# The seven products of the last feed-forward matrix: order of sums, casts and transfers

## Chip, cores and metric

The kernel runs on one core of a Trainium2 chip. The metric is device time in microseconds, from three runs of each kernel; one more execution was profiled.

## What is computed

One decoder layer on x (1024 tokens by 1024), with the float32 products each made of three passes over two parts of the operands.

```python
def rms_norm(x, g):
    y = x * rsqrt(mean(x * x, axis=-1, keepdims=True) + EPS)
    return y * g

def swiglu(x, w_in, w_out):
    a, b = split(x @ w_in, 2, axis=-1)
    return (silu(a) * b) @ w_out

h = x
h = h + stick_breaking_attention(rms_norm(h, norm_mix), sb_w_in, sb_w_out)
h = h + swiglu(rms_norm(h, norm_ffn), ffn_w_in, ffn_w_out)
gate = sigmoid(rms_norm(h, norm_ple) @ ple_w_gate)
h = h + gate * (p @ ple_w_proj)
out = rms_norm(h, final_norm)
```

The change lies in the product with `ffn_w_out` (2816 by 1024), the sum into h behind it, and the start of the product with `ple_w_gate`.

## The kernel before

Activations are kept transposed, 128 features on the partitions and tokens along the row. A float32 operand is used as two parts: the *high* part is a cast to fp32r on ScalarE, the *low* part is the value less the high part, a subtraction on VectorE or GpSimd. `mm3` (L118) makes a product of three matmuls: high by high (L119), high by low (L120), low by high (L121).

The product with `ffn_w_out` is made as one step of a fast two-by-two scheme: seven products P1, P5, P6, P7, P2, P4, P3 (`FO`, L611), in this order, instead of eight. A product takes sums and differences of quarters of the matrix and of the activations, and has 11 pieces along the inner dimension (`NJ`), so there are 77 pieces, numbered n (`NS`). A piece is a 128 by 1024 tile: 512 columns of weights beside 512 of activations. Each piece is used by 12 matmuls of 512 columns (four row blocks, three parts), which add into four banks of PSUM.

From here on the order on each engine is that in which the program is written (`manual_schedule`, L608). Step n of the loop (L1071) writes, in this order:

- `fo_load(n + 6)` (L622): two transfers on SyncE's queue, weights (L620) and activations (L642), 256 KB each. Buffers of `NG` = 7 names rotate; in P4 three of them (`4 + j % 3`), since the others are about to hold the residual stream.
- `fo_lo(n + 2)` (L675): the difference of piece n+2 on VectorE (L684; L682 in P1).
- `fo_hi(n + 3)` (L644): for P5, P6 and P7 the sum or difference of quarters on VectorE, 128 by 1024 (L652), for P4 and P3 of one half only, none for P1 and P2; then the cast on ScalarE (L672; L670 in P1).
- at steps of P2 that `gate_split` lists, `w_split` (L90) of a gate weight: the cast (L100) on ScalarE and the difference (L102) on VectorE, for the last three weights on GpSimd; at steps that `gate_load` lists, `w_load` (L82) of a gate weight on SyncE's queue (L87). Raw gate weights alternate between two buffers.
- the matmuls of piece n, and one or two *jobs* from a list.

The high and low parts of pieces and of the later gate weights come from a pool of 16 tiles (`xp`, tag "X"), two of which are taken all the time.

Jobs are added at a product's last piece. `evac_fo` (L1039) takes a product's four banks into the residual stream `hres`: P1 and P5 with copies on ScalarE (L1044, L1046), the others with additions on VectorE (L1034); P7 has three of them for each bank. `residual` (L1036) is a transfer on GpSimd's queue that adds 256 KB of the stream before the feed-forward part into `hres`: four behind P6, twelve behind P7. After P2 and P4, `parts3(m, 0)` (L1014) is a job for each of eight row blocks: it casts the block, scaled by the gain, on ScalarE (L1022), takes the difference on VectorE (L1023), squares the block on ScalarE (L1029; L1026 for the first) and adds the square to `acc3` (L1031), on VectorE for odd m and on GpSimd for even m.

After the loop: the gate weights that are not yet split (`w_next`, L107: load, split, two further loads, a split ahead), and for the first 512 tokens the gate products (L1163), eight row blocks of 24 matmuls; in the first block `parts3(m, 1)` of the second half for four m, and the sums of squares (`stats_sum`, L124), whose result is spread over the partitions by transposes on TensorE (L149) after the second block, before the first gate block can be finished.

Of the kernel before, what the change touches and what calls it, by code (L numbers as in the profile page):

```python
# [34 lines left out]
def f(ap):  # L35
    return ap.bitcast(F32)
# [3 lines left out]
def tile_trunk(ctx: ExitStack, tc: tile.TileContext, xT, pT, gains, ident, w_qkv, w_o, w_fi, w_fo, w_g, w_p, outT):  # L40
# [46 lines left out]
            nc.sync.dma_start(t[:, :n, :], src)  # L87
            raws[k] = t

    def w_split(k):  # L90
        if k < lim[0] and k in raws:
            n = order[k][1]
            t = raws.pop(k)
            if len(order[k]) > 2 and order[k][2]:
                hi = xp.tile([P, T], F32R, name=f"whi{k}", tag="X").rearrange("p (k m) -> p k m", k=KT)
                lo = xp.tile([P, T], F32R, name=f"wlo{k}", tag="X").rearrange("p (k m) -> p k m", k=KT)
            else:
                hi = wp.tile([P, KT, P], F32R, name=f"whi{k}", tag="whi", bufs=2)
                lo = wp.tile([P, KT, P], F32R, name=f"wlo{k}", tag="wlo", bufs=2)
            nc.scalar.copy(hi[:, :n, :], t[:, :n, :])  # L100
            eng = nc.gpsimd if k < N1 or k >= len(order) - 3 else nc.vector
            eng.tensor_tensor(lo[:, :n, :], t[:, :n, :], f(hi[:, :n, :]), op=ALU.subtract)  # L102
            parts[k] = (hi, lo)

    cur = [0]

# [498 lines left out]
    def tmp(name):  # L605
        return pt.tile([P, 512], F32, name=name, tag="t")
# [403 lines left out]
        return hh[h][kt][:, cs], hl[h][kt][:, cs]  # L1010

    begun = set()

    def parts3(m, h):  # L1014
        hs = HS[h]
        g = gn[:, 2, m:m + 1]
        if h or m < 7:
            d = p3.tile([P, 2, 512], F32R, name=f"g_{m}_{h}", tag=f"s{m}" if h else f"g{m}", bufs=1)
        else:
            d = duo(xp, "g_7_0", "X", None)  # L1020
        hh[h][m], hl[h][m] = d[:, 0, :], d[:, 1, :]
        nc.scalar.activation(hh[h][m], hres[m][:, hs], AF.Copy, scale=g)  # L1022
        nc.vector.scalar_tensor_tensor(hl[h][m], hres[m][:, hs], g, f(hh[h][m]), op0=ALU.mult, op1=ALU.subtract)  # L1023
        if h not in begun:
            begun.add(h)
            nc.scalar.activation(acc3[:, hs], hres[m][:, hs], AF.Square)  # L1026
        else:
            s = tmp("sq")
            nc.scalar.activation(s, hres[m][:, hs], AF.Square)  # L1029
            eng = nc.vector if m % 2 else nc.gpsimd  # L1030
            eng.tensor_tensor(acc3[:, hs], acc3[:, hs], s, op=ALU.add)  # L1031

    def plus(out, x, y, op=ALU.add):
        nc.vector.tensor_tensor(out, x, y, op=op)  # L1034
# [4 lines left out]
    def evac_fo(p, i, ps):  # L1039

        c11, c12 = hres[i][:, HS[0]], hres[i][:, HS[1]]
        c21, c22 = hres[i + 4][:, HS[0]], hres[i + 4][:, HS[1]]
        if p == "P1":
            nc.scalar.copy(c11, ps)  # L1044
        elif p == "P5":
            nc.scalar.copy(c22, ps)  # L1046
        elif p == "P6":
            plus(c21, ps, c11)
            residual(i, 0)
        elif p == "P7":  # L1050
            plus(c12, c21, c22, ALU.subtract)
            residual(i, 1)
            plus(c21, ps, c21, ALU.subtract)
            plus(c22, c21, c22)
            residual(i + 4, 1)
            residual(i + 4, 0)
        elif p == "P2":
            plus(c11, ps, c11)
        elif p == "P4":
            plus(c21, ps, c21)  # L1060
        else:
            plus(c12, ps, c12)

    gate_load = {("P6", 8): 0, ("P7", 4): 1, ("P2", 1): 2, ("P2", 3): 3, ("P2", 5): 4, ("P4", 1): 5, ("P4", 2): 6}
    gate_split = {("P2", 1): 0, ("P2", 3): 1, ("P2", 5): 2, ("P2", 7): 3, ("P2", 9): 4}
    n_wg = len(gate_split)
    jobs = []
    for n in (3, 4, 5):
        fo_load(n)
# [1 line left out]
    for n in range(NS):  # L1071
        p, j = FO[n // NJ], n % NJ
        fo_load(n + 6)
        if n < 3:
            nc.sync.dma_start(SX[n][:, 1, :], act_d[n][0])
        if 5 <= n < 5 + NJ:
            fo_w(SX[n - 5][:, 0, :], n - 5, 1, 1)
        fo_lo(n + 2)
        fo_hi(n + 3)
        if (p, j) in gate_split:  # L1080
            w_split(n_fi + gate_split[(p, j)])
        if (p, j) in gate_load:
            w_load(n_fi + gate_load[(p, j)])
        if j == 0:
            pm = [mb() for _ in range(4)]
        hi, lo = fop.pop(n)
        for i in range(4):
            ws = slice(i * P, i * P + P)
            mm3(pm[i], hi[:, 0, ws], lo[:, 0, ws], hi[:, 1, :], lo[:, 1, :], j == 0, j == NJ - 1)
        if n in (2, 5):  # L1090
            rests.pop(0)()
        if j == NJ - 1:
            jobs += [lambda p=p, i=i, ps=ps: evac_fo(p, i, ps) for i, ps in enumerate(pm)]
            more = {"P2": range(4), "P4": range(4, KT)}
            jobs += [lambda m=m: parts3(m, 0) for m in more.get(p, ())]
        elif j:
            left = NJ - 1 - j
            for _ in range(1 if len(jobs) <= left else 2):
                if jobs:
                    jobs.pop(0)()  # L1100
# [58 lines left out]
    for ri, (c0, n) in enumerate(ranges):  # L1159
# [3 lines left out]
        for m in range(KT):  # L1163
            wh, wl = wg[m]
            ple_load(ri * KT + m + 2)
            ps = mb()
            for kt in range(KT):
                mm3(ps[:, :n], wh[:, kt, :], wl[:, kt, :], *gx(kt, c0, n), kt == 0, kt == KT - 1)

            def evac(ri=ri, m=m, c0=c0, n=n, ps=ps):  # L1170
                evac_g(ps, m, c0, n, pls.pop(ri * KT + m), ri == last)
                if ri == last:
                    nc.scalar.activation(hg[m], hres[m][:, c0:c0 + n], AF.Copy, scale=gf[:, m:m + 1])

            held.append(evac)
            if (ri, m) == (0, 0):
                parts3(0, 1)
                parts3(1, 1)
                y3 = stats_sum(cp, mb(), [acc3[:, HS[0]], None], 0, 4)
                parts3(2, 1)  # L1180
                parts3(3, 1)
            elif (ri, m) == (0, KT - 1):
                y3 = stats_sum(cp, mb(), [None, acc3[:, HS[1]]], 512, 4)
            if ri < 2 and m == 1:
                stats_spread(mb(), y3, rstd3, 512 * ri, 4)
            if m or ri == last:
                while held:
                    held.pop(0)()
            if ri == 0 and 1 < m < 6:
                parts3(m + 2, 1)  # L1190
            if before is not None:
                b0, bn = before
                s = 4 if ri == last else 5
                if m == s - 2:
                    yfin = stats_sum(cp, mb(), acc4, b0, bn // P)
                elif m == s:
                    rfin = spread(yfin, bn // P)
                if m >= s:
                    for q in range(3 * (m - s), min(3 * (m - s) + 3, KT)):
                        fin(q, b0, bn, rfin)  # L1200
# [44 lines left out]
```

## Time and profile before

| | us |
|---|---|
| median of three runs | 1393.1 (1392.13 to 1393.51) |
| the profiled execution | 1391.86 |
| its span, first to last instruction | 1389.9 |
| TensorE busy | 1343.3 |
| VectorE busy | 1076.6 |
| ScalarE busy | 626.3 |
| GpSimd busy | 408.8 |
| mean granted clock of TensorE | 0.99 |

All times of rows are in microseconds from the span's start unless marked otherwise; PE is TensorE, DVE VectorE, ACT ScalarE, POOL GpSimd, SP SyncE (SPq and POOLq their queues). L12 is line 12 of the kernel. Matmuls overlap: a row of 0.39 us is followed by the next matmul 0.227 us later when nothing is missing. The granted clock is a share of full speed.

### The profile page before, as it was taken

What the parts mean: (1) busy time and instruction counts of PE and PEld (TensorE: products, weight loads), DVE (VectorE), ACT (ScalarE), POOL (GpSimd) and SP (SyncE); (2) the same over time, 40 slices, a digit from 0 to 9 for tenths busy, and PEclk for the clock granted to TensorE, in tenths of its full rate; (3) what the DMA queues carried; (4) which work ended last, traced back from release to release, by engine and by line L of the source; (5) the groups of instructions that cost most, each with busy time, mean ns of one, the idle gap of its engine ahead of it and who ended that gap; (6) DMA issues with size and microseconds to landing.
All of it is one profiled execution on the core that took longest, in us unless ns stands there. A gap on an engine that the chain in (4) does not pass through costs nothing. (4 is left out here: it accounts for less than half of the span.)

```text
span 1389.9 us, 17597 instructions
## 1 busy us (share of the span) xinstructions
PE 1343.3 (97%) x6506; PEld 1112.2 (80%) x6506; DVE 1076.6 (77%) x1379; ACT 626.3 (45%) x1091; POOL 408.8 (29%) x289
## 2 busy tenths in 40 slices
PE   9999999999999999999999999999999889888996
PEld 7888888888888888888888888888888667666896
DVE  6878878887887876687888888888896678667775
ACT  6666565556656754443232332232253325244433
POOL 2222231213223401245544454544420002002321
PEclk9999999999999999999999999999999999999998
DMA  5101110111111742532122221222168457761113
GB/s 187 58 16 61 46 47 31 46 46 46 46 47 61 252 180 91 175 122 82 57 89 91 91 91 61 77 91 91 61 228 308 147 176 207 221 243 50 34 66 109
DMA packets 65877, 146.98 MB, mean 106 GB/s; under 512 B 7168, under 2 KB 11648, under 8 KB 65792
## 3 DMA queue, kind: packets, MB, share of 16 engines
q1 hardware_dynamic: 61200, 134.06, 28.0%
q0 software_dynamic: 4320, 11.54, 3.3%
q8 instruction: 51, 0.84, 0.3%
q14 instruction: 34, 0.28, 0.1%
q10 hardware_dynamic: 272, 0.26, 0.1%
HBM read 114.38 MB, written 31.46 MB: 105 GB/s over the span
## 5 line engine op out<-in xcount | busy, mean ns | idle before, releaser
L413 DVE TENSOR_TENSOR_SCAN a<-a,hot 128x128 f32<-128x128 f32 (+7 forms) x128 | 193.1, 1524 | 21.9 <-ACT a L406 21.5
L119 PE MATMUL b_pj<-xh,whi 128*128 128x512 f32 x352 | 140.6, 399 | 0.0
L121 PE MATMUL b_pj<-xh,wlo 128*128 128x512 f32 x352 | 138.7, 394 | 0.4 <-POOL wlo L102 0.4
L120 PE MATMUL b_pj<-xl,whi 128*128 128x512 f32 x352 | 137.8, 392 | 0.0
L102 POOL TENSOR_TENSOR wlo<-wraw,whi 128x1024 fp32r<-128x1024 f32 x27 | 67.5, 2501 | 225.5 <-ACT whi L100 130.5
L436 DVE TENSOR_TENSOR al<-b_tp,ah 128x512 fp32r<-128x512 f32 (+2 forms) x160 | 93.2, 599 | 52.1 <-ACT ah L435 51.7
L435 ACT CAST ah<-b_tp 128x512 fp32r<-128x512 f32 (+2 forms) x160 | 81.9, 521 | 79.9 <-PE b_tp L426 79.1
L406 ACT ACTIVATE a<-b_z 128x128 f32<-128x128 f32 (+2 forms) x192 | 86.9, 490 | 49.2 <-PE b_z L404 48.2
L120 PE MATMUL b_m<-fl,fh 128*128 128x512 f32 x231 | 94.0, 407 | 11.2 <-DVE fl L684 11.0
L426 PE MATMUL b_tp<-hot,a 128*128 128x128 f32 x576 | 94.2, 273 | 2.5 <-DVE al L436 2.5
L426 PEld LDWEIGHTS b_tp<-hot,a 128*128 128x128 f32 x576 | 72.6, 140 | 25.8 <-DVE al L436 5.6
L121 PE MATMUL b_m<-fh,fl 128*128 128x512 f32 x231 | 91.8, 397 | 0.0
L119 PE MATMUL b_m<-fh 128*128 128x512 f32 x231 | 91.8, 397 | 0.0
L121 PEld LDWEIGHTS b_pj<-xh,wlo 128*128 128x128 f32 x352 | 66.0, 188 | 16.2 <-POOL wlo L102 0.5
L120 PEld LDWEIGHTS b_pj<-xl,whi 128*128 128x128 f32 x352 | 66.2, 188 | 8.9
L119 PEld LDWEIGHTS b_pj<-xh,whi 128*128 128x128 f32 x352 | 66.1, 188 | 8.6
L446 PE MATMUL b_av<-ah,V 128*128 128x512 f32 (+2 forms) x160 | 70.7, 442 | 0.0
L672 ACT CAST fh<-s 128x1024 fp32r<-128x1024 f32 x33 | 34.7, 1050 | 78.2 <-DVE s L652 65.8
L120 PEld LDWEIGHTS b_m<-fl,fh 128*128 128x128 f32 x231 | 44.2, 191 | 29.8 <-DVE fl L684 20.7
L684 DVE TENSOR_TENSOR fl<-s,fh 128x1024 fp32r<-128x1024 f32 x33 | 42.6, 1290 | 32.1 <-ACT fh L672 32.1
L672 ACT CAST fh<-raw 128x1024 fp32r<-128x1024 f32 x33 | 34.0, 1049 | 69.6 <-DVE raw L652 56.1
L894 ACT ACTIVATE sg<-u 128x512 f32<-128x512 f32 x22 | 13.9, 632 | 106.1 <-issue 91.4
(3066 smaller groups left out, 3883.4 us busy)
## 6 DMA issues: line engine op xcount, KB each, us to landing
fraw<-w_fi SPq DMA_DIRECT2D x44, 512.0 KB, 4.1
raw<-w_fo SPq DMA_DIRECT2D x56, 256.0 KB, 3.5
raw<-act SPq DMA_DIRECT2D x55, 256.0 KB, 3.6
wraw<-w_qkv SPq DMA_DIRECT2D x22, 512.0 KB, 3.5
sp<-hl SPq DMA_DIRECT2D x14, 512.0 KB, 3.1
act<-u SPq DMA_DIRECT2D x22, 256.0 KB, 2.2
act<-c SPq DMA_DIRECT2D x22, 256.0 KB, 2.6
s<-act SPq DMA_DIRECT2D x22, 256.0 KB, 5.4
```

The lines of the kernel that those rows point to most:

```text
L102: eng.tensor_tensor(lo[:, :n, :], t[:, :n, :], f(hi[:, :n, :]), op=ALU.subtract)
L119: nc.tensor.matmul(ps, whi, xhi, start=first, stop=False)
L120: nc.tensor.matmul(ps, whi, xlo, start=False, stop=False)
L121: nc.tensor.matmul(ps, wlo, xhi, start=False, stop=last)
L406: nc.scalar.activation(a[:, c0:c0 + e], z[:, :e], AF.Sigmoid, scale=-SCALE)
L413: nc.vector.tensor_tensor_scan(a[:, L - 1::-1], a[:, L - 1::-1], hot[:, back], 0.0, op0=ALU.mult, op1=ALU.max)
L426: nc.tensor.transpose(b[:, j * P:(j + 1) * P], a[:, kt * P:(kt + 1) * P], idn)
L435: nc.scalar.copy(ah[:, m0:m0 + 512 - j0 * P], b[:, j0 * P:])
L436: nc.vector.tensor_tensor(al[:, m0:m0 + 512 - j0 * P], b[:, j0 * P:], f(ah[:, m0:m0 + 512 - j0 * P]), op=ALU.subtract)
L446: nc.tensor.matmul(ps[:, c0:], o.V[:, kt, hd, :], ah[:, r0:], start=kt == 0, stop=False)
L672: nc.scalar.copy(hi, d)
L684: nc.vector.tensor_tensor(lo, d, f(hi), op=ALU.subtract)
```

## The change

Five edits, all in the seven products and the start of the gate stage:

- step n writes `fo_hi(n + 3)` ahead of `fo_lo(n + 2)`;
- `parts3` is cut in two: casts and squares on ScalarE, then difference and addition on VectorE (`parts3_lo`), which comes one job later, beside the casts of the next row block (`parts3_row`: five jobs for four blocks, nine pieces for the eight of the second half). All additions of squares are VectorE's;
- `residual(i, 1)` moves from P7's evacuation to P2's, `residual(i + 4, 1)` to P4's;
- the loads of gate weights stand further apart, five instead of seven in the stage; three weights instead of five are split in it, cast and difference one step apart; five instead of three weights have their difference on GpSimd;
- the first gate block takes the pieces of the second half from the same list.

```diff
-    def w_split(k):
+    def w_hi(k):
         if k < lim[0] and k in raws:
...
             nc.scalar.copy(hi[:, :n, :], t[:, :n, :])
-            eng = nc.gpsimd if k < N1 or k >= len(order) - 3 else nc.vector
+            parts[k] = (hi, lo, t)
+
+    def w_lo(k):
+        if k < lim[0] and k in parts and len(parts[k]) == 3:
+            n = order[k][1]
+            hi, lo, t = parts[k]
+            eng = nc.gpsimd if k < N1 or k >= len(order) - 5 else nc.vector
             eng.tensor_tensor(lo[:, :n, :], t[:, :n, :], f(hi[:, :n, :]), op=ALU.subtract)
             parts[k] = (hi, lo)
+
+    def w_split(k):
+        w_hi(k)
+        w_lo(k)
...
         nc.scalar.activation(hh[h][m], hres[m][:, hs], AF.Copy, scale=g)
-        nc.vector.scalar_tensor_tensor(hl[h][m], hres[m][:, hs], g, f(hh[h][m]), op0=ALU.mult, op1=ALU.subtract)
         if h not in begun:
             begun.add(h)
             nc.scalar.activation(acc3[:, hs], hres[m][:, hs], AF.Square)
         else:
-            s = tmp("sq")
-            nc.scalar.activation(s, hres[m][:, hs], AF.Square)
-            eng = nc.vector if m % 2 else nc.gpsimd
-            eng.tensor_tensor(acc3[:, hs], acc3[:, hs], s, op=ALU.add)
+            squares[(m, h)] = tmp("sq")
+            nc.scalar.activation(squares[(m, h)], hres[m][:, hs], AF.Square)
+
+    def parts3_lo(m, h):
+        hs = HS[h]
+        g = gn[:, 2, m:m + 1]
+        nc.vector.scalar_tensor_tensor(hl[h][m], hres[m][:, hs], g, f(hh[h][m]), op0=ALU.mult, op1=ALU.subtract)
+        if (m, h) in squares:
+            nc.vector.tensor_tensor(acc3[:, hs], acc3[:, hs], squares.pop((m, h)), op=ALU.add)
+
+    def parts3_row(ms, h):
+
+        ms = list(ms)
+
+        def piece(a, b):
+            if b is not None:
+                parts3(b, h)
+            if a is not None:
+                parts3_lo(a, h)
+
+        return [lambda a=a, b=b: piece(a, b) for a, b in zip([None] + ms, ms + [None])]
...
             plus(c12, c21, c22, ALU.subtract)
-            residual(i, 1)
             plus(c21, ps, c21, ALU.subtract)
             plus(c22, c21, c22)
-            residual(i + 4, 1)
             residual(i + 4, 0)
         elif p == "P2":
             plus(c11, ps, c11)
+            residual(i, 1)
         elif p == "P4":
             plus(c21, ps, c21)
+            residual(i + 4, 1)
...
-    gate_load = {("P6", 8): 0, ("P7", 4): 1, ("P2", 1): 2, ("P2", 3): 3, ("P2", 5): 4, ("P4", 1): 5, ("P4", 2): 6}
-    gate_split = {("P2", 1): 0, ("P2", 3): 1, ("P2", 5): 2, ("P2", 7): 3, ("P2", 9): 4}
-    n_wg = len(gate_split)
+    gate_load = {("P6", 8): 0, ("P7", 4): 1, ("P2", 6): 2, ("P4", 3): 3, ("P3", 1): 4}
+    gate_hi = {("P2", 1): 0, ("P2", 4): 1, ("P2", 9): 2}
+    n_wg = len(gate_hi)
...
+        fo_hi(n + 3)
         fo_lo(n + 2)
-        fo_hi(n + 3)
-        if (p, j) in gate_split:
-            w_split(n_fi + gate_split[(p, j)])
+        if (p, j - 1) in gate_hi:
+            w_lo(n_fi + gate_hi[(p, j - 1)])
+        if (p, j) in gate_hi:
+            w_hi(n_fi + gate_hi[(p, j)])
...
-            jobs += [lambda m=m: parts3(m, 0) for m in more.get(p, ())]
+            jobs += parts3_row(more[p], 0) if p in more else []
...
             if (ri, m) == (0, 0):
-                parts3(0, 1)
-                parts3(1, 1)
+                rest3 = parts3_row(range(KT), 1)
+                for _ in range(3):
+                    rest3.pop(0)()
                 y3 = stats_sum(cp, mb(), [acc3[:, HS[0]], None], 0, 4)
-                parts3(2, 1)
-                parts3(3, 1)
+                for _ in range(2):
+                    rest3.pop(0)()
...
             if ri == 0 and 1 < m < 6:
-                parts3(m + 2, 1)
+                rest3.pop(0)()
```

## Rows read from the trace of the kernel before

**Rows 1.** The page, busy time, share of the span and instructions of each engine.

```profile
PE 1343.3 (97%) x6506; PEld 1112.2 (80%) x6506; DVE 1076.6 (77%) x1379; ACT 626.3 (45%) x1091; POOL 408.8 (29%) x289
```

**Rows 2.** Busy time by stretch: P1, P5, P6, P7, P2, P4, P3 (stretch, length, engines).

```profile
core 0: us, PE busy (x) PEld busy (x) DVE busy (x) ACT busy (x) POOL busy (x), PEclk, DMA share, GB/s
1025.30:1055.30 30.00, 30.00 (x134) 24.77 (x133) 25.87 (x39) 16.10 (x25) 0.00 (x0) 1.00 0.99 351
1055.30:1087.40 32.10, 30.72 (x133) 24.51 (x132) 21.50 (x19) 11.43 (x14) 0.00 (x0) 1.00 0.71 251
1087.40:1126.30 38.90, 33.27 (x133) 23.92 (x133) 26.07 (x23) 13.50 (x15) 0.00 (x0) 1.00 0.49 159
1126.30:1165.80 39.50, 33.27 (x133) 23.92 (x133) 29.53 (x28) 14.40 (x15) 3.55 (x4) 1.00 0.65 184
1165.80:1195.80 30.00, 30.00 (x134) 24.82 (x134) 24.28 (x27) 11.71 (x12) 10.62 (x12) 1.00 0.99 246
1195.80:1240.80 45.00, 35.55 (x133) 27.52 (x132) 27.96 (x33) 17.06 (x20) 1.25 (x1) 0.89 0.78 270
1240.80:1281.10 40.30, 34.71 (x133) 24.80 (x132) 28.79 (x30) 16.95 (x20) 5.65 (x4) 0.96 0.04 14
```

**Rows 3.** Waits in the seven products: who, for whom, us in total, times, longest.

```profile
PE b_pj L120 <- DVE fl L684: 15.3, 18, 2.8
...
PE b_m L120 <- DVE fl L684: 11.0, 15, 2.3
```

**Rows 4.** Timeline in P6: start, length, engine, line, what [idle before, for whom].

```profile
1118.90 1.23 DVE L684 TENSOR_TENSOR fl<-s,fh 128x1024 fp32r<-128x1024 f32 x1 [1.17 <-ACT fh L672]
1120.04 1.22 DVE L652 TENSOR_TENSOR s<-raw,s 128x1024 f32<-128x1024 f32 x1
...
1121.35 1.05 ACT L672 CAST fh<-s 128x1024 fp32r<-128x1024 f32 x1 [2.48 <-DVE s L652]
...
1122.43 1.23 DVE L684 TENSOR_TENSOR fl<-s,fh 128x1024 fp32r<-128x1024 f32 x1 [1.17 <-ACT fh L672]
```

**Rows 5.** Timeline of TensorE: the first matmuls of P1, P5 and the gate stage.

```profile
1025.32 0.39 PE L119 MATMUL b_m<-fh 128*128 128x512 f32 x1
...
1055.27 0.39 PE L119 MATMUL b_pj<-fh 128*128 128x512 f32 x1
...
1281.12 0.39 PE L119 MATMUL b_pj<-g,whi 128*128 128x512 f32 x1
```

**Rows 6.** Groups of instructions in the seven products: count | busy, mean ns | idle before.

```profile
L1034 DVE TENSOR_TENSOR h<-b_m,h 128x512 f32<-128x512 f32 x12 | 8.2, 686 | 0.3
...
L102 POOL TENSOR_TENSOR wlo<-wraw,whi 128x1024 fp32r<-128x1024 f32 x2 | 5.4, 2723 | 0.7 <-ACT whi L100 0.7
```

**Rows 7.** Timeline of VectorE before P2: five differences in a row.

```profile
1161.94 5.77 DVE L684 TENSOR_TENSOR fl<-raw,fh 128x1024 fp32r<-128x1024 f32 x5 [1.24 <-ACT fh L672]
```

**Rows 8.** Timeline of TensorE: the first matmuls of P4's first and third piece.

```profile
1195.77 0.39 PE L119 MATMUL b_pj<-fh 128*128 128x512 f32 x1
...
1208.59 0.63 PE L119 MATMUL b_pj<-fh 128*128 128x512 f32 x1
```

**Rows 9.** Line L642 (loads of activations), 1168 to 1200, seven transfers.

```profile
DMA to landing us min/median/max: 6.3/10.5/14.8
```

**Rows 10.** The same line in P4, 1203 to 1222, six transfers.

```profile
DMA to landing us min/median/max: 3.0/3.7/4.6
```

**Rows 11.** Timeline of VectorE at the end of P4.

```profile
1224.25 0.75 DVE L1023 SCALAR_TENSOR_TENSOR g<-h,gn,g 128x512 fp32r<-128x512 f32 x1 [1.78 <-ACT g L1022]
1224.92 1.22 DVE L684 TENSOR_TENSOR fl<-raw,fh 128x1024 fp32r<-128x1024 f32 x1
...
1234.24 2.29 DVE L684 TENSOR_TENSOR fl<-raw,fh 128x1024 fp32r<-128x1024 f32 x1
```

**Rows 12.** Timeline of ScalarE at the start of the gate stage.

```profile
1284.43 1.05 ACT L100 CAST whi<-wraw 128x1024 fp32r<-128x1024 f32 x1 [5.48 <-DMA wraw<-w_g]
1285.39 0.72 ACT L1022 ACTIVATE g<-h,gn 128x512 fp32r<-128x512 f32 x1
```

**Rows 13.** Timeline of TensorE: the transposes after the second gate block.

```profile
1292.96 0.60 PE L149 MATMUL b_m<-hot,st_y 128*128 128x128 f32 x4
```

More of the change, by code (lines that the diff above doesn't have):

```diff
@@ L1012, in tile_trunk @@
     begun = set()
+    squares = {}
     def parts3(m, h):
```

## Prediction

> **What bounds the kernel now.** I read the page's busy line first: TensorE is busy 97% of the span [rows 1]. That is a mean over stages, so the next view is the busy time by product of the last feed-forward matrix, the stage that nearly all of the diff touches [rows 2]. Two products, P1 and P2, take 30 us each; the other five, with the same 132 matmuls, take 32.1 to 45.0. The first matmuls of P1, of P5 and of the gate stage [rows 5] give the measure: P1 took 1055.27 - 1025.32 = 29.95 us with TensorE never idle, which is 2.72 us for each of its 11 pieces, and all seven took 1281.12 - 1025.32 = 255.8 us. Seven at P1's pace would be 209.6. So **46.2 us** are lost here: about 2.2 in P5, 8.9 in P6, 9.6 in P7, 15.1 in P4, 10.4 in P3 (each its length less 29.95). The waits show who is late: TensorE waits for the low half of an operand, made by VectorE at L684 [rows 3]. These two groups are only 26 us; the rest is the pace of matmuls after a wait, at a granted clock of 0.89 in P4 and 0.96 in P3 [rows 2], the lower level of 1.2 GHz for part of those stretches.
>
> Why VectorE is late stands in one cycle of the timeline [rows 4]: difference at 1118.90, sum of the next piece at 1120.04, the cast of that sum on ScalarE at 1121.35, and the next difference only at 1122.43, when the cast is done. VectorE works 1.14 + 1.14 us and then stands 1.2 us: 3.53 us a piece where TensorE needs 2.72. It is a loop of two engines that take turns, not a full engine: VectorE is busy 26 of 39 us in P6 [rows 2].
>
> **The change, part by part.**
>
> *Sum in front of the difference.* VectorE now does sum(n+3), difference(n+2), sum(n+4), difference(n+3). The cast of n+3 starts after its sum and has a difference and another sum, 2.28 us, to finish its 1.05 us plus some 0.15 of handing over. The wait goes and a piece costs VectorE 2 x 1.14 = 2.28 us, under TensorE's 2.72. For this VectorE must issue back to back: five differences in a row took 5.77 us [rows 7], one start every 1.14. The Trainium skill (VectorE: DVE Perf Modes, The DRAIN you can't avoid) says that after each operation the engine is flushed for about its duration less 0.27 us before the next starts. By that, read on top of the 1.22 us of a row, an estimated 2 x (1.22 + 0.95) = 4.3 us a piece would keep VectorE the bound and take the whole gain; rows 7 speak against it here. Per product VectorE then needs: P5, P6 11 x 2.28 = 25.1 us; P7 the same and four evacuations at 0.60 (a row's 0.69 [rows 6] less the overlap of 0.08 that rows 7 show); P2 11 x 1.14, four evacuations of P7 with three operations each (8 us), three gate differences (3.4) and the first sums of P4: 26; P4 and P3 a half-wide sum, 11 x (1.14 + 0.60), four evacuations and four pieces of the residual stream at 0.67 + 0.60: 26.6 at most. All lie under 29.95, so TensorE becomes the bound in all seven. **Gain 46.2 us**, if nothing else is late.
>
> What is queued behind the moved sum: it waits for the loads of piece n+3, and the difference of n+2, which needs no load, now stands behind it. In P5 to P2 seven buffers keep loads some six pieces ahead. In P4 only three rotate, and the load of n+3 is issued when difference n ends. From there to sum n+3 VectorE has two pieces' time less a sum and a difference, so a piece takes at least (0.60 + 1.22 + 0.5 + landing) / 2, the 0.5 being my allowance for handing over and issuing two transfers; with the quiet landing of 3.7 us [rows 10] 3.0 us. VectorE comes into P4 with four pieces prepared and ends the last difference about 3.4 + 6 x 3.0 = 21 us (the first of them at 3.4, six more at this pace) after TensorE starts P4; TensorE wants it at 27.2. Hidden, by 6 us.
>
> *Residual stream a piece ahead.* Before, a piece's cast, its low half and its sum stand in one job, so VectorE waits 1.78 us for ScalarE, with the difference that TensorE needs queued behind it [rows 11]. Now the casts go one job earlier: that wait goes too, eight times in the stage; it is part of the 46.2. All additions of squares go to VectorE: three more of 0.60 in this stage, three in the gate stage, against two 1.14 us differences that leave. With GpSimd's addition beside it VectorE's difference took 2.29 us instead of 1.22 [rows 11]; that goes as well. Counted in the sums above, net nothing.
>
> *Eight of the sixteen residual transfers* move from P7's evacuation to P2's and P4's. At that place the load of the activations took 6.3 to 14.8 us to land, median 10.5 [rows 9], with the transfer engines 0.99 busy in P2 and 0.04 in P3 [rows 2]; and P4's first two steps took 1208.59 - 1195.77 = 12.8 us instead of 5.4 [rows 8]. A residual is as large as one half of a piece's load, so eight fewer leave P2 room for four pieces' loads. On GpSimd's queue nothing else stands behind them in these products but an addition that the change removes. The cover is P2's evacuation, six pieces ahead of P4's tight loads: bounds for what remains of the hand-over are 0 and the old 7.4 us; I take 1, near 0, since the loads that were late are the ones unburdened. SyncE's queue gains too: gate loads 2 to 4 are issued three or more pieces after their buffer is free, and no longer hold the product's loads behind them.
>
> *Gate weights.* Three instead of five are split in the stage; weights 3 to 7 are split after it, the low halves on GpSimd at 2.72 us [rows 6]. Two raw buffers alternate, so weights 5 and 7 wait for a low half and a load. Before, one such round stood there: ScalarE waited 5.48 us for the last weight [rows 12] before it cast it and came to the second half of the residual stream. Now there are two rounds, one longer by 2.72 + 3.7 + 1.05 = 7.4 us, and TensorE's transposes of the statistics [rows 13] wait for what is behind. The cover: ScalarE and VectorE end P3 some 5 us ahead of TensorE (with its last eight sums VectorE has 24.8 of 29.95 us to do), where before they ended it behind. Bounds 0 and 7.4; I take 1, nearer 0, because the row behind it has a stretch of TensorE-bound P3 in front.
>
> **Sum.** The profiled execution took 1391.86 us (span 1389.9). 1391.86 - 46.2 + 1 + 1 = 1347.7. The median of the runs is 1.2 above the profiled one: **1348.9 us**.
>
> **Rivals.**
> 1. *The loads stay late at P4.* If they land in 10.5 us [rows 9] through P4, the three buffers give (2.3 + 10.5) / 2 = 6.4 us a piece, the last difference at 3.4 + 6 x 6.4 = 41.8 us, 14.6 after it is wanted: 1346.9 (the forecast without its two allowances) + 14.6 = 1361.5. For it: 12 residuals made that landing. Against: four remain there.
> 2. *The gate stage starts behind ScalarE's late casts*, all 7.4 us: 1354.3. For it: the round is real and ScalarE works in order. Against: it begins while TensorE still has products to do.
> 3. *The change doesn't do what it says*: VectorE's pair does not come under 2.72 (a wait between sum and difference that the trace of before can't show), and only P4 and P3 gain, 25.5 of the 46.2: 1367.6.
> 4. *VectorE is held after each operation for as long again*, a mechanism of 2 x 2.44 = 4.9 us a piece in P5 to P7: 33 x (4.9 - 2.72) = 72 us, 1419, **slower**. Rows 7 show the opposite. The page on VectorE named above would put it at an estimated 1401.
> 5. *The sum blocks the difference in P4 for good*, **slower**: place, the three buffers; price, the formula of rival 1. At a landing of 21 us a piece takes 11.7 us, the last difference comes at 73 and the 46 us are gone; at 22 it is 1396. The longest landing of rows 9 is 14.8, so it would take more crowding than before with fewer transfers there.
>
> **How the numbers follow.** Chances: forecast 0.67, rival 1 0.13, rival 2 0.12, rival 3 0.04, rival 4 0.01, rival 5 0.02, and 0.01 that several of them cancel the gain. A measurement of this kernel can tell about 0.2% (2.8 us) from no change. The forecast and rivals 1 to 3 are faster: 0.96; same 0.01; slower 0.03. The range reaches from 1345 (no allowance used, less the spread of the runs) to 1362 (rival 1) and holds the first three cases, about 0.9.
>
> **What would show it.** Right: P5, P6 and P7 at 30 us each in the busy time by product; the wait of L684 for ScalarE nearly gone; no row of TensorE waiting for L684; the granted clock 1.00 in P4 and P3; loads of activations landing in 3 to 6 us around P2. Wrong: a wait of VectorE's sum (L652) for a load in P4, or a gap of TensorE before the transposes of L149 with ScalarE casting gate weights at that time. A stage above 225 us would mean that the loop of two engines was not the cause.

## The result and the profile after

The kernel after takes 1346.68 us (median of four runs, 1345.97 to 1347.7), beside 1393.3 for the kernel before in the same session (1392.13 to 1393.51): a ratio of 0.9668, 95% interval 0.9651 to 0.9684. The profiled execution took 1345.97 us with a span of 1344.2, 45.7 less than before. (One of the six runs of the last experiment below took 1362.62 us at a mean granted clock of 0.93, and makes its interval wide.)

The lines of the loop have moved in the kernel after: the sum is L662 (was L652), the cast L682 (L672), the difference L694 (L684), the loads of activations L652 (L642), the cast and difference of the stream L1033 and L1044 (L1022 and L1023), the transposes L159 (L149).

The busy line of the page, answering to [rows 1]:

```profile
PE 1325.3 (99%) x6506; PEld 1110.3 (83%) x6506; DVE 1067.2 (79%) x1383; ACT 627.0 (47%) x1091; POOL 406.0 (30%) x285
```

Busy time by stretch, P1, P5, P6, P7, P2, P4, P3 and the gate stage (columns as in [rows 2]):

```profile
1025.10:1055.50 30.40, 30.40 (x134) 24.57 (x133) 28.41 (x42) 16.68 (x26) 0.00 (x0) 1.00 0.98 354
1055.50:1085.40 29.90, 29.90 (x134) 24.75 (x133) 29.90 (x28) 16.68 (x20) 0.00 (x0) 1.00 0.97 348
1085.40:1115.30 29.90, 29.90 (x133) 24.77 (x132) 24.52 (x23) 11.75 (x13) 0.61 (x1) 1.00 0.64 210
1115.30:1145.20 29.90, 29.90 (x133) 24.77 (x132) 22.61 (x23) 16.25 (x16) 3.04 (x5) 1.00 0.79 229
1145.20:1175.10 29.90, 29.90 (x133) 24.76 (x132) 22.92 (x26) 8.33 (x8) 10.61 (x12) 1.00 0.91 206
1175.10:1205.10 30.00, 30.00 (x134) 24.82 (x134) 24.19 (x31) 14.50 (x18) 0.00 (x0) 1.00 0.80 278
1205.10:1235.00 29.90, 29.90 (x134) 24.75 (x133) 29.29 (x33) 16.42 (x20) 6.39 (x3) 1.00 0.33 113
1235.00:1344.20 109.20, 96.52 (x629) 87.86 (x627) 69.03 (x162) 39.01 (x77) 26.54 (x24) 0.95 0.24 78
```

All seven products take 30 us, TensorE is never idle in them, and the granted clock is 1.00 in P4 and P3, which had 0.89 and 0.96. The five products that took 32.1 to 45.0 us [rows 2] now take what P1 takes. By their first matmuls the seven took 209.9 us instead of 255.8 [rows 5]:

```profile
1025.07 0.39 PE L129 MATMUL b_m<-fh 128*128 128x512 f32 x1
...
1234.99 0.39 PE L129 MATMUL b_pj<-g,whi 128*128 128x512 f32 x1
```

From there to the end the span is 109.2 us, before 108.8. So next to nothing of the gain is given back: 45.9 us less in the products, 0.25 less ahead of them, 0.4 more behind.

VectorE early in P5, the cycle that answers to [rows 4]:

```profile
1057.87 1.22 DVE L662 TENSOR_TENSOR s<-s,raw 128x1024 f32<-128x1024 f32 x1
1059.01 1.22 DVE L694 TENSOR_TENSOR fl<-s,fh 128x1024 fp32r<-128x1024 f32 x1
1060.14 1.22 DVE L662 TENSOR_TENSOR s<-s,raw 128x1024 f32<-128x1024 f32 x1
```

A sum, a difference and the next sum with no bracket of idle time: 2.27 us a piece, under TensorE's 2.72. In P5 VectorE is busy all the time and runs ahead; later something else stops it. The waits in the seven products (who, for whom, us in total, times, longest):

```profile
ACT fh L682 <- DVE raw L662: 43.7, 16, 9.0
...
DVE raw L662 <- DMA raw<-act: 12.4, 7, 3.7
...
ACT fh L682 <- PE b_m L131: 7.6, 6, 1.7
...
ACT fh L682 <- PE b_pj L131: 4.5, 3, 1.7
```

No wait of TensorE's matmuls for L694 is among them, where there were 26 us [rows 3], and no wait of the difference for the cast. Instead ScalarE waits for TensorE (7.6 and 4.5 us), 6.9 of them in P7 and 4.0 in P2: I read this as the pool of tiles being full of pieces that TensorE has not used. Before, it waited so for 7.9 us, in P5 and P2, and not once in P6 and P7. That is the mark of a producer that is ahead; I call the distance the *lead*. VectorE's sum does wait for loads, 12.4 us in all, and no matmul of TensorE waits because of it.

### The profile page after: what moved, and what is told of

Its sections match the earlier page's. It is cut to its first block, busy times and chain, and to the rows that moved or that the text cites. A ratio compares the mean times of both kernels' runs of the same rounds, so it can differ in the third digit from the quotient of the medians.

```text
span 1344.2 us, 17635 instructions
## 1 busy us (share of the span) xinstructions
PE 1325.3 (99%) x6506; PEld 1110.3 (83%) x6506; DVE 1067.2 (79%) x1383; ACT 627.0 (47%) x1091; POOL 406.0 (30%) x285
## 4 chain that ended last, share of the span: by engine, by line
PE 82%; DVE 9%; DMA 3%; issue 2%; ACT 2%; POOL 1%; SPq 0%; DVEq 0%; ACTq 0%; POOLq 0%
PE b_m L129 13%; PE b_m L130 13%; PE b_m L131 13%; PE b_pj L129 10%; PE b_pj L130 9%; PE b_pj L131 9%; PE b_tp L436 4%; DVE a L423 3%; PE b_av L457 2%; PE b_av L456 2%; DMA raw<-act 2%; PE b_z L413 2%; PE b_z L414 2%; DVE fl L694 1%; DVE QA L291 1%
## 5 line engine op out<-in xcount | busy, mean ns | idle before, releaser
L108 POOL TENSOR_TENSOR wlo<-wraw,whi 128x1024 fp32r<-128x1024 f32 x29 | 72.2, 2491 | 289.3 <-ACT whi L100 195.7
L130 PE MATMUL b_m<-fl,fh 128*128 128x512 f32 x231 | 90.0, 390 | 0.0
L682 ACT CAST fh<-raw 128x1024 fp32r<-128x1024 f32 x33 | 34.4, 1054 | 60.7 <-DVE raw L662 43.7
L457 PE MATMUL b_av<-al,V 128*128 128x512 f32 (+2 forms) x160 | 57.7, 361 | 0.2 <-DVE al L446 0.2
L906 DVE TENSOR_TENSOR u<-q,u 128x512 f32<-128x512 f32 x22 | 36.7, 1667 | 26.1 <-POOL u L900 26.1
L1064 POOL DMA_DIRECT2D h<-h x16 | 14.3, 1531 | 131.6 <-DVE h L1061 129.4
```

What stands on the lines that cost most here:

```text
L130: nc.tensor.matmul(ps, whi, xlo, start=False, stop=False)
L457: nc.tensor.matmul(ps[:, c0:], o.V[:, kt, hd, :], al[:, r0:], start=False, stop=last)
L906: nc.vector.tensor_tensor(cb, ca, cb, op=ALU.mult)
```

## The experiments

Times are medians; every difference from the kernel before is against runs on the same chip (1393.04, 1393.57 and 1393.29 in the three sessions, beside 1393.3 above), so that kernels of different sessions can be compared to about 1.5 us. Runs 1 to 4 divide the change into its parts.

**Run 1, the kernel before with the swap alone.**

```diff
-        fo_lo(n + 2)
         fo_hi(n + 3)
+        fo_lo(n + 2)
```

> The kernel before with one edit: the sum of piece n+3 in front of the difference of n+2. Theory (the loop of VectorE and ScalarE is the cause): P5, P6 and P7 fall to 30 us each, 20.7 us together, P3's first eight pieces lose their 3.05 us pace (2.6 us), the hand-over from P2 to P4 and the jobs of the residual stream stay late: 1365 to 1370 us. Rival (the spread of transfers and jobs decides, the order of sum and difference matters little): over 1383 us, P6 and P7 still above 36 us.

1351.72 us, ratio 0.9703 (0.9689 to 0.9718). Two lines give 41.3 of the 46.6 us, more than I expected. Busy time by stretch in P6, P4 and P3:

```profile
1086.10:1116.00 29.90, 29.90 (x134) 24.75 (x133) 24.36 (x23) 11.63 (x13) 0.64 (x1) 1.00 0.64 210
1175.80:1209.40 33.60, 31.16 (x134) 24.46 (x132) 25.95 (x32) 15.10 (x18) 1.33 (x1) 1.00 0.79 262
1209.40:1240.40 31.00, 30.22 (x133) 24.70 (x132) 28.79 (x30) 16.97 (x20) 6.50 (x4) 1.00 0.21 75
```

P5, P6 and P7 are full, as all theories had it. The surprise is P4: 33.6 us, where I had expected it above 40, though all twelve residual transfers stand where they stood and the loads around P2 landed in 2.9/9.4/11.9 us (minimum, median, maximum). The hand-over from P2 to P4, 7.4 us before, is gone with the swap: P4's first two pieces take 5.4 us, and VectorE comes to them with pieces in hand. What is left to lose stands in P4's last four pieces and P3's first.

**Run 2, the kernel after without the swap.**

```diff
-        fo_hi(n + 3)
         fo_lo(n + 2)
+        fo_hi(n + 3)
```

> The kernel after without that one edit, the difference again in front of the sum. Theory: P5, P6 and P7 go back to 32, 39 and 39.5 us, P3 to about 3.05 us a piece, the rest keeps its gain: 1368 to 1373 us. Rival (the spread decides): under 1357 us.

1381.38 us, ratio 0.9914 (0.9899 to 0.9929): all the other edits together give 12 us. P6 and P4 by stretch:

```profile
1086.90:1125.80 38.90, 33.35 (x133) 23.94 (x133) 26.08 (x23) 13.48 (x15) 0.00 (x0) 1.00 0.49 161
...
1195.20:1225.40 30.20, 30.20 (x133) 24.70 (x132) 21.76 (x27) 13.71 (x17) 0.00 (x0) 1.00 0.83 266
```

and TensorE's waits in the gate stage:

```profile
PE b_m L159 <- DVE st_y L154: 8.3, 1, 8.3
```

P6 is what it was before. P4 is mended here too, without the swap, and P3 takes 33.6 us; but TensorE waits 8.3 us before the transposes of L159, the place of my second rival, and from the first gate matmul to the end the run takes 120.3 us instead of 109.2. So P4's and P3's losses have two remedies, each of which suffices for most of them (20.7 us by run 1, 21.5 by run 2), and the gains of the parts can't be added. Only the swap mends P5 to P7.

**Run 3, the kernel after with all twelve residuals behind P7.**

```diff
             plus(c12, c21, c22, ALU.subtract)
+            residual(i, 1)
             plus(c21, ps, c21, ALU.subtract)
             plus(c22, c21, c22)
+            residual(i + 4, 1)
...
             plus(c11, ps, c11)
-            residual(i, 1)
...
             plus(c21, ps, c21)
-            residual(i + 4, 1)
```

> The kernel after with all twelve residual transfers behind P7 again. Theory as in the prediction: the loads for P4 land late again, at 10 us instead of 5, and P4 loses part of its old 7.4 us: 1349 to 1355 us. Rival (with VectorE ahead of TensorE the late loads are hidden): 1346 to 1348 us, loads landing late all the same.

1346.19 us, ratio 0.9662 (0.9645 to 0.9678): no difference from the kernel after, and all seven products are full. The landing of the activations' loads around P2:

```profile
DMA to landing us min/median/max: 3.0/6.9/13.6
```

against 3.1/4.9/8.4 in the kernel after, and VectorE's waits for them in this run:

```profile
DVE raw L662 <- DMA raw<-act: 12.6, 9, 4.8
```

The transfers do crowd the loads, as [rows 9] let one think, and up to 13.6 us of landing is hidden by the lead. The theory that the hand-over needs the spread fell.

But this run asks less than its edit says. GpSimd's transfers in the kernel after:

```profile
1156.17 7.21 POOL L1064 DMA_DIRECT2D h<-h  x8 [2.54 <-DVE h L1061]
```

With three ahead of these eight and one behind, all twelve are issued in P2 there too, none in P4 (GpSimd in the stretches above: x12 in P2, x0 in P4). Each adds into a part of `hres` that P7's evacuation wrote, and nothing on GpSimd's queue holds back the eight that the program writes behind P2's and P4's evacuations. The edit spreads the issues from P2's start to 18.4 us behind it, where this run has them from 5.8 us ahead of it to 11.6 behind. What eight fewer transfers in P2 would be worth is not shown by it.

**Run 4, the kernel after with the stream's cast, difference and addition in one job.**

```diff
-        return [lambda a=a, b=b: piece(a, b) for a, b in zip([None] + ms, ms + [None])]
+        def whole(m):
+            parts3(m, h)
+            parts3_lo(m, h)
+
+        return [lambda m=m: whole(m) for m in ms]
...
-                for _ in range(3):
+                for _ in range(2):
                     rest3.pop(0)()
```

> The kernel after with cast, square, difference and addition of a row block of the residual stream in one job again, all additions still on VectorE. Theory: VectorE waits about 1.8 us for ScalarE in each of eight jobs with TensorE's difference behind it, a piece takes it some 4.8 us where TensorE needs 2.7; part of that eats the lead and the rest shows: 1349 to 1358 us. Rival (the lead covers it): 1346 to 1348 us.

1352.29 us, ratio 0.9708 (0.9693 to 0.9722), 5.6 above the kernel after. The number came as I expected, at another place: all seven products are full, and the loss stands in the gate stage. TensorE's waits there:

```profile
PE b_m L159 <- DVE st_y L154: 4.5, 1, 4.5
```

The last gate weight's cast and the first cast of the second half behind it, on ScalarE, in this run:

```profile
1243.90 1.05 ACT L100 CAST whi<-wraw 128x1024 fp32r<-128x1024 f32 x1 [3.38 <-DMA wraw<-w_g]
1244.85 0.72 ACT L1033 ACTIVATE g<-h,gn 128x512 fp32r<-128x512 f32 x1
```

and in the kernel after:

```profile
1239.94 1.05 ACT L100 CAST whi<-wraw 128x1024 fp32r<-128x1024 f32 x1 [3.20 <-DMA wraw<-w_g]
1240.89 0.72 ACT L1033 ACTIVATE g<-h,gn 128x512 fp32r<-128x512 f32 x1
```

TensorE starts the gate stage at the same time in both (1234.7 and 1235.0); ScalarE, which works in order, comes 4 us later to the second half. The transposes need the squares of the first half only. But VectorE works in order too, and has the second half's first differences and an addition in front of the statistics of the first half, so these wait with it for ScalarE's casts. VectorE in this run and, below it, in the kernel after:

```profile
1245.60 3.02 DVE L1044 SCALAR_TENSOR_TENSOR g<-h,gn,g 128x512 fp32r<-128x512 f32 x2 [9.76 <-ACT g L1033]
```

```profile
1241.64 3.03 DVE L1044 SCALAR_TENSOR_TENSOR g<-h,gn,g 128x512 fp32r<-128x512 f32 x2 [5.76 <-ACT g L1033]
```

After the wait the clock is lower too:

```profile
1246.00:1256.00 10.00, 5.52 (x20) 4.32 (x20) 8.96 (x20) 4.72 (x9) 1.41 (x1) 0.83 0.01 2
```

The granted clock (0.83) is the eighth column; after the wait of 4.5 us part of this stretch ran at the lower level of 1.2 GHz.

**Runs 5 to 8** ask what the small edits do together. Run 5 is the kernel after with the gate weights loaded and split as before (7 loads and 5 splits in the stage), run 6 that and run 4's edit, run 7 the kernel before with run 1's edit and the change's second and fifth (the stream's pieces), run 8 the kernel before with run 1's edit and the moved residuals (run 3's lines the other way round). Run 5's edit:

```diff
-            eng = nc.gpsimd if k < N1 or k >= len(order) - 5 else nc.vector
+            eng = nc.gpsimd if k < N1 or k >= len(order) - 3 else nc.vector
...
-    gate_load = {("P6", 8): 0, ("P7", 4): 1, ("P2", 6): 2, ("P4", 3): 3, ("P3", 1): 4}
-    gate_hi = {("P2", 1): 0, ("P2", 4): 1, ("P2", 9): 2}
+    gate_load = {("P6", 8): 0, ("P7", 4): 1, ("P2", 1): 2, ("P2", 3): 3, ("P2", 5): 4, ("P4", 1): 5, ("P4", 2): 6}
+    gate_split = {("P2", 1): 0, ("P2", 3): 1, ("P2", 5): 2, ("P2", 7): 3, ("P2", 9): 4}
...
-        if (p, j - 1) in gate_hi:
-            w_lo(n_fi + gate_hi[(p, j - 1)])
-        if (p, j) in gate_hi:
-            w_hi(n_fi + gate_hi[(p, j)])
+        if (p, j) in gate_split:
+            w_split(n_fi + gate_split[(p, j)])
```

> The kernel after with the loads and splits of the gate weights as before: five splits in the stage, three late ones, the last three low halves on GpSimd. Theory (the two late rounds of gate weights sit right at the limit in the kernel after): the wait before the transposes of L159, 0.2 us, goes, the seven products stay full, 1346 to 1347 us, no difference that can be measured. Rival (the two more splits and their loads crowd P2 and P4): over 1350 us.

> The run with the stream in one job (1352.3 us) and, in addition, the gate weights as before. Theory (that run's 5.6 us are TensorE's wait for the statistics behind ScalarE's late casts, not VectorE's waits in the products): the wait goes, 1346 to 1348 us. Rival (VectorE's waits in P4 and P3 cost it): 1351 to 1353 us.

> The kernel before with two edits: the sum in front of the difference, and the residual stream's casts a job ahead with all its additions on VectorE. Transfers and gate weights as before. Theory (these two edits are the whole gain): 1346 to 1348 us, all seven products at 30 us. Rival (the transfers are needed too): P4 over 31 us, 1349 to 1353 us.

> The kernel before with two edits: the sum in front of the difference, and eight residual transfers moved from P7 to P2 and P4. Stream and gate weights as before. Theory (the 4.8 us that the swap alone loses in P4 and at P3's start come from the stream's jobs, some of them on GpSimd): P4 stays at 33 us, 1350 to 1352 us. Rival (they come from loads that land late behind twelve residual transfers): P4 at 30 us, 1346 to 1348 us.

| run | us | ratio, interval | P4 | P3 | wait at L159 |
|---|---|---|---|---|---|
| after | 1346.68 | 0.9668 (0.9651 to 0.9684) | 29.9 | 29.9 | 0.2 |
| 5 | 1347.9 | 0.9673 (0.9659 to 0.9688) | 31.3 | 30.5 | none |
| 6 | 1351.87 | 0.9701 (0.9685 to 0.9717) | 33.7 | 31.0 | none |
| 7 | 1348.55 | 0.9677 (0.9662 to 0.9691) | 31.1 | 30.5 | none |
| 8 | 1349.89 | 0.9685 (0.967 to 0.9699) | 31.2 | 31.0 | none |

P4 by stretch in run 6:

```profile
1175.90:1209.60 33.70, 31.49 (x133) 24.41 (x132) 23.91 (x31) 14.04 (x17) 0.00 (x0) 1.00 0.80 268
```

Run 6 was to show that run 4's loss is one of the gate start alone. It did not: with the gate start relieved, the same 5 us came back as lost time in P4 and P3. Runs 4 and 11 have the same one-job pieces and full products, so these cost the products nothing there; here, with the gate weights split early as well, they do. Run 8 beside run 1 shows the moved residuals worth 1.8 us (P4 31.2 instead of 33.6), against nothing in run 3, and neither of its theories came out whole. In run 8 four transfers do leave P2: GpSimd's additions of the stream, which the kernel after has on VectorE, stand ahead of them, and they are issued 26.8 us into P4. In run 6 all twelve are issued in P2, and P4 takes 33.7. Runs 5 and 7 are within 2 us of the kernel after, at the edge of what can be told: the loss stands in P4's later pieces and P3's first, so run 5's theory of full products fell.

**Run 9** asks how the early gate splits of run 5 cost P4 2 us. It leaves every load, cast and difference of the kernel after in its place, but takes the four tiles of gate weights 3 and 4 from the pool of 16 in P2, by a copy of one column on GpSimd.

```diff
...
+    def w_early(k):
+        two = [xp.tile([P, T], F32R, name=f"{n}{k}", tag="X") for n in ("whi", "wlo")]
+        for t in two:
+            nc.gpsimd.tensor_copy(t[:, 0:1], ones)
...
+        if (p, j) in (("P2", 7), ("P2", 9)):
+            w_early(n_fi + (3 if j == 7 else 4))
```

> The kernel after, but the four tiles of gate weights 3 and 4 are taken from the pool of 16 at P2's eighth and tenth piece, as the early splits of before took them; their loads, casts and differences stay late. Theory (early splits cost P4 because they leave fewer tiles for pieces prepared ahead): P4 and P3's start lose about 2 us as in the run with the gate weights as before, 1348 to 1350 us. Rival (the early loads crowd P4's loads): P4 stays at 30 us, 1346 to 1347 us.

1351.22 us, ratio 0.97 (0.9687 to 0.9712). P4 and P3 by stretch:

```profile
1176.50:1208.40 31.90, 31.10 (x134) 24.47 (x132) 21.44 (x27) 13.64 (x17) 0.00 (x0) 1.00 0.83 251
1208.40:1238.90 30.50, 30.50 (x133) 24.62 (x132) 30.50 (x35) 16.26 (x21) 5.28 (x2) 1.00 0.39 139
```

and TensorE's wait at the gate start (here L168):

```profile
PE b_m L168 <- DVE st_y L163: 2.5, 1, 2.5
```

P4 and P3 lose 2.6 us beside run 5's 2.0. But the tiles are not all that changed. GpSimd's copies wait for tiles to come free, and eight of the twelve residual transfers queue behind them, 5 to 8 us later in P2 than in the kernel after:

```profile
1165.95 0.18 POOL L86 CAST whi<-ones 128x1 fp32r<-128x1 f32 x1 [5.50 <-PE b_pj L140]
1166.42 7.19 POOL L1073 DMA_DIRECT2D h<-h  x8 [0.17 <-issue]
```

In P2 VectorE then waits 2.6 us before a difference and 1.5 before a gate weight's until TensorE is done with a tile, and 5.5 us for a load early in P4 (the longest such wait in the kernel after is 3.7). Run 5 has both too: its casts of gate weights wait 7.1 us for tiles, and VectorE's sum once 6.2 us for a load. So taken tiles do hold VectorE up, but how much of the 2 us is theirs, and how much that of late loads, is not shown. I had not counted that the shorter lead shows at the gate start as well, another 2.5 us.

**Run 10** tests the bound itself: two VectorE additions of 512 columns, which nobody reads, with each prepared piece of P5 to P7 of the kernel after.

```diff
+        if n + 3 < NS and FO[(n + 3) // NJ] in ("P5", "P6", "P7"):
+            if n + 3 == NJ:
+                scr = tmp("scr")
+            for q in range(2):
+                nc.vector.tensor_tensor(scr, hot[:, HS[q]], hot[:, HS[q]], op=ALU.add)
```

> The kernel after with two more additions of 128x512 on VectorE in each piece of P5, P6 and P7 (1.2 us a piece, on data that nobody waits for). Theory (VectorE's 2.28 us a piece only has to stay under TensorE's 2.72): with 3.48 us a piece VectorE is the bound again, P6 and P7 at some 38 us, 1363 to 1369 us. Rival (the turn-taking of the two engines was the cause and VectorE has room): under 1352 us.

1378.41 us, ratio 0.9893 (0.9881 to 0.9906). VectorE in P6 and P6 by stretch:

```profile
1099.66 1.22 DVE L662 TENSOR_TENSOR s<-raw,s 128x1024 f32<-128x1024 f32 x1
1100.79 1.22 DVE L694 TENSOR_TENSOR fl<-s,fh 128x1024 fp32r<-128x1024 f32 x1
1101.93 1.41 DVE L1111 TENSOR_TENSOR scr<-hot 128x512 f32<-128x512 f32 x2
1103.26 1.22 DVE L662 TENSOR_TENSOR s<-raw,s 128x1024 f32<-128x1024 f32 x1
```

```profile
1090.30:1129.90 39.60, 33.62 (x133) 23.91 (x132) 39.22 (x45) 13.39 (x16) 0.00 (x0) 1.00 0.46 146
```

A piece takes VectorE 1.13 + 1.14 + 1.33 = 3.60 us, and TensorE's pieces in P6 come every 3.60. I had put the two additions at 1.2 us; they took 1.33, and P7's evacuations came on top (41.1 us). P4 and P3 (31.3 and 30.5) and a wait of 2.4 us at the gate start add the rest of the miss. P6 is as long as before the change (38.9), yet VectorE is busy 39.2 of 39.6 us where it was busy 26: one is an engine that is full, the other a loop that waits for itself.

**Runs 11 and 12** move the casts of gate weights 5 to 7 behind the first pieces of the stream's second half, in run 4's kernel (11) and in the kernel after (12).

```diff
-    while len(wg) < KT:
-        wg.append(w_next())
+    wg.append(w_next())
+    wg.append(w_next(False))
...
                     rest3.pop(0)()
+                while len(wg) < KT:
+                    wg.append(w_next())
```

> The run with the stream in one job (1352.3 us, all seven products full, 4.5 us of TensorE's wait before the transposes of L159), with the casts of gate weights 5 to 7 behind the first pieces of the stream's second half. Theory (that wait is ScalarE's queue, and is the whole 5.6 us): the wait goes, 1346 to 1348 us. Rival (the wait has another cause, or comes back later as a wait for the evacuations): over 1350 us.

> The kernel after with the same move of the casts of gate weights 5 to 7. Theory: the 0.2 us before L159 go and nothing else does, 1345.5 to 1347 us, no difference that can be measured against the kernel after. Rival (the late weights, now later by some 6 us, hold up the gate products): 1349 us or more.

Run 11 took 1348.18 us, ratio 0.9674 (0.9662 to 0.9687): 4.1 of run 4's 5.6 us are back, so most of run 4's loss was ScalarE's order of work at the gate start. TensorE's new waits there:

```profile
PE b_pj L137 <- DVE acc L1171: 1.0, 1, 1.0
PE b_m L137 <- DVE acc L1046: 0.7, 1, 0.7
```

Run 12 took 1346.24 us (1345.81 to 1362.62), ratio 0.9684 (0.9648 to 0.9719): its wait at L159 is gone, and it can't be told from the kernel after, whose wait there is 0.2 us. No version beat the kernel after by more than the runs scatter.

## Why the prediction was right, step by step

**The bound.** Right as put: two engines that take turns. The swap alone gives 41.3 of 46.6 us (run 1), the rest without it 12 (run 2), and VectorE's pair takes 2.27 us in the profile after against the 2.28 foreseen. Run 10 shows the other side: at 3.60 us a piece VectorE bounds TensorE again.

**The rival that VectorE is held after each operation.** Not borne out: in P5 operations of 1.22 us start every 1.14 us, in run 10 too, and a hold as long as the operation would have made P6 longer than 2.72 us a piece. The Trainium skill (VectorE: DVE Perf Modes, The DRAIN you can't avoid), read as the prediction read it, does not hold for these operations; the same section says that a next operation that is not held starts earlier, which is what these rows show. The measurement decides.

**Sum.** Forecast 1347.7 for the profiled execution, measured 1345.97. The gain in the products was 45.9 instead of 46.2: the six products after P1 took 29.92 us each, and P1 took 30.4, 0.46 more than before, in its first two pieces. That was not foreseen. It shows in most kernels with the swap (30.1 to 30.45) and not in runs 4, 8 and 11 (29.92 to 29.95). In the profile after, TensorE's weight loads wait there 0.9 us for VectorE, 0.6 of them for differences, and not at all in the profile before; why VectorE is later there is open. Of the two allowances of 1 us neither was needed in full: the seven products show no hand-over, and the gate start waits 0.2 us:

```profile
PE b_m L159 <- DVE st_y L154: 0.2, 1, 0.2
```

**The hand-over from P2 to P4.** The time came right, but not for the reason given, and that is luck. The prediction took the 7.4 us as cured by the unburdened loads, and 1 as what remains. The swap alone removes them (run 1). The step that failed is "eight fewer leave P2 room": all twelve transfers are still issued in P2 (run 3), so rival 1 was also wrong to count four there. What unburdened loads would be worth stays open; run 8, where four transfers do leave, gains 1.8 us. "Loads of activations landing in 3 to 6 us" failed with it: around P2 they took 3.1/4.9/8.4. Those issued in P4, when the transfers were through, took 3.0/3.2/5.6, so rival 1's 10.5 did not come. VectorE's sum waited for loads in P4, 7.0 us in five waits, which the prediction had named as the sign of being wrong. The end of P4's sums and differences in the profile after:

```profile
1176.70 1.22 DVE L694 TENSOR_TENSOR fl<-raw,fh 128x1024 fp32r<-128x1024 f32 x1
...
1194.88 0.69 DVE L662 TENSOR_TENSOR raw<-raw,s 128x512 f32<-128x512 f32 x1 [2.68 <-DMA raw<-act]
...
1198.49 1.22 DVE L694 TENSOR_TENSOR fl<-raw,fh 128x1024 fp32r<-128x1024 f32 x1
```

The first and the last line are the first and the eighth difference after P4's start: (1198.49 - 1176.70) / 7 = 3.1 us a piece, close to the 3.0 foreseen, in spite of the waits. But VectorE came into P4 with three pieces prepared, not four, after waiting 5.5 us for loads in P2. So P4's last difference is ready at 1199.71, 24.6 us after P4's first matmul at 1175.15 (foreseen 21), and wanted at 27.2. 2.6 us of the foreseen 6 were left: hidden, by less than I said. A wait was the wrong sign; the lead that it leaves is the right one.

**The residual stream.** "Net nothing" beside the gain was wrong at two places. The edit is worth 5.6 us in this kernel (run 4), at the gate start, where the prediction looked for none, and 3.2 on top of the swap alone, in P4 and P3 (runs 1 and 7). And VectorE's slowing beside GpSimd does not go with GpSimd's additions: it goes on beside the low halves of gate weights (next section). In P3 VectorE was busy 29.3 us, where I had 26.6 at most.

**The gate weights.** The allowance of 1 measured 0.2, and its cover (engines that end P3 ahead of TensorE) was the right one: without the swap the wait is 8.3 us (run 2), near the bound of 7.4, and 4.5 and 2.5 in runs 4 and 9. Rival 2 was a real place with about the right price, and the cover that holds it is thin: VectorE ended P3's work ahead of its evacuations 2.5 us before TensorE (1232.54 and 1234.99), not 5. What the prediction missed is that this edit also helps P4 and P3, by about 2 us (run 5): it leaves four tiles to the pieces and moves loads out of P2. Which of the two does it is not shown (run 9 changes both).

**Rival 3** (VectorE's pair stays above 2.72 us, only P4 and P3 gain) did not come. Run 2, in which the pair is undone, shows what it looks like: P5 to P7 as before, P4 and P3 with 21.5 us of the 25.5 that the rival gave them, and 8.3 of that lost again at the gate start.

## What to carry to other kernels

When an engine that is far from full is late all the same, look in its timeline for a producer and a consumer of the same engine with another engine's step between them, and write the next piece's producer ahead of the consumer. Afterwards count the lead, not the waits: how many prepared pieces the buffers hold, who takes buffers from them, how late their loads land, and how far ahead the producer is where the next stage's work queues behind it in order. A transfer that is written later in the program is not issued later unless something on its queue holds it; look when it was issued. Edits that cure the same lateness by different ways don't add up; test each alone and all but each.

## What was not expected of the hardware

VectorE beside GpSimd. At the end of P3 in the profile after, GpSimd and VectorE:

```profile
1226.65 5.34 POOL L108 TENSOR_TENSOR wlo<-wraw,whi 128x1024 fp32r<-128x1024 f32 x2 [62.13 <-ACT whi L100]
1233.95 2.40 POOL L108 TENSOR_TENSOR wlo<-wraw,whi 128x1024 fp32r<-128x1024 f32 x1 [1.96 <-ACT whi L100]
```

```profile
1226.86 2.88 DVE L1044 SCALAR_TENSOR_TENSOR g<-h,gn,g 128x512 fp32r<-128x512 f32 x1
1229.66 2.88 DVE L1046 TENSOR_TENSOR acc<-acc,sq 128x512 f32<-128x512 f32 x1
1233.15 2.05 DVE L1061 TENSOR_TENSOR h<-b_m,h 128x512 f32<-128x512 f32 x3 [0.61 <-PE b_m L131]
```

The first two read two tensors of SBUF and took 2.88 us beside GpSimd's differences, against 0.75 and 0.68 elsewhere; the evacuations, which read one tensor from PSUM, kept 0.68 beside the third. The Trainium skill (GPSIMD Engine Reference, Key points) has such contention for VectorE instructions with two SBUF inputs; these rows agree. The rows of before have it too, 2.29 us for L684 at 1234.24 [rows 11], beside an addition on GpSimd that ran 1.25 us from 1234.20. In run 12 it hit even an operation of four columns, L145, in the chain of the statistics:

```profile
1242.16 1.48 DVE L144 TENSOR_SCALAR st_y<-st_v 128x4 int32<-128x4 int32 x1
1243.67 2.31 DVE L145 TENSOR_TENSOR st_y<-magic,st_y 128x4 int32<-128x4 int32 x1
```

L145 takes 0.16 us in the kernel after and 2.31 here, beside two low halves on GpSimd (1241.22 to 1245.96). L144 in front of it reads one tensor only and took 1.48 instead of 0.17, which two inputs do not explain; its cause is open. So work that is moved to an idle GpSimd can cost VectorE as long as GpSimd takes. Runs 1 and 5 to 8 took two of the five late low halves from GpSimd and none took all, so what that would be worth at the gate start was not tried.
